# Where the conditioning sums of the last layer run in a four-layer decoder trunk

## The chip, the cores and the metric

The kernel runs on one core of one Trainium2 chip. The metric is the device time of one execution in microseconds (us), as a median of several runs. "PE" is the engine that multiplies matrices, "PEld" its weight loads, "DVE" the vector engine, "ACT" the scalar engine, "POOL" the general engine and "SP" the engine whose queue issues most DMAs. Each engine works through its own instructions in a fixed order; where an instruction waits for another engine, everything behind it on the same engine waits too.

## What is computed

Four layers, each with one token mixer, work on x of 1024 positions by 1024 features, all in 32-bit floats. Ahead of each mixer the input is normalised, scaled and shifted, and behind it the result is multiplied by a gate; scale, shift and gate of a layer come from one conditioning vector c:

```python
for i in range(DEPTH):                                  # DEPTH = 4
    mod = (c @ ada_w[i] + ada_b[i])[:, None, :]         # 1024 -> 3 * 1024
    shift, scale, gate = jnp.split(mod, 3, axis=-1)
    h = rmsnorm(x, norm_g[i]) * (1.0 + scale) + shift
    kind = i % N_MIXERS                                 # 0, 1, 2, 0
    if kind == 0:   y = hgrn2_mixer(h, ...)             # layers 0 and 3
    elif kind == 1: y = swa_mixer(h, ...)               # layer 1
    else:           y = gdn_mixer(h, ...)               # layer 2
    x = x + gate * y
```

The product `c @ ada_w[i]` is what this case calls the conditioning sums of layer i. Layer 0 is HGRN2 (a gated recurrence), layer 1 attention within a window of 128 positions, layer 2 gated DeltaNet, layer 3 HGRN2 again.

## The kernel before

Each layer projects h with large matrix products, mixes, and projects back. A product of two 32-bit floats is made of three passes (L222, L223, L224: high by high, low by high, high by low parts), so each weight tile is loaded from memory by SP (`w_raw`, L191), rounded to its high part on ACT (`w_hi`, L193) and subtracted on DVE to get its low part (`w_lo`, L194). The tiles `w_raw` lie in a pool of three buffers, tagged `raw`.

The conditioning sums are made by `ada(i, parts)`. The 3072 outputs of a layer are cut into 6 parts of 512. For each part eight tiles of 128 by 512 weights are loaded (`ada_w`, 256 KB each, L462, into the same three `raw` buffers), multiplied by the fitting column of c and added up on DVE (`ada_acc`: one TENSOR_SCALAR, L446, then seven SCALAR_TENSOR_TENSOR, L448). DVE then transposes the sum in blocks (L466, into a `raw` buffer again) and reduces it (L467, `ada_red`). When the parts of a call are done, one small product on PE (L470) puts the sums in place in a bank of PSUM, `ada_ps`, and DVE adds the bias from there into `mod` (L474, four instructions, and L492 for the scales). That bank has the tag `tr`, of which there is one; the transposes of the mixers (`kh_ps`, `qt_ps`, `ktr_ps` and others) use the same one bank. The generator `ada` yields after each of the eight loads and after each part, so a part has 9 steps and a half layer (3 parts) 27.

The order of the work around these steps comes from `weave`, which interleaves several generators by estimated shares of the time, and after that from a scheduler that places each engine's instructions by the order written, by what is ready by its estimate, and by which buffers are free. The conditioning sums of the next layer are the stream `side` of the present layer, woven with its mixing and its projections. The table `NS` says how many steps a weave takes:

```python
# hgrn2, for each head h but the last; the first takes 18
weave(self.tc, (mix(h, ds[h]), 16000, 0, 1, PRH), (g, tot, 0, 1, 0), (take(side, ns), ns, 0, 1, 0))
# swa, for each group g of four heads but the last (three times), then what is left
weave(self.tc, (mix(g, ds[g]), 28000, 0, 1, PRS), (chain(proj_q(g + 1, ds[g + 1]), proj_z(g + 1, ds[g + 1])), 42000, 0, 1, 0), (take(side, NS[1]), NS[1], 0, 1, 0))
drain(side)
# gdn, for each pair of heads u (eight times)
weave(self.tc, *st_, (chain(*cs), tot, 0, 1, 0), (take(side, NS[2]), NS[2], 0, 1, 0))
```

In the attention layer `mix(g)` goes through eight blocks of positions. Of each block it transposes the queries into `qt_ps` (L1467, tag `tr`), copies them out on ACT (L1470, L1471, `sw_qhi`) and DVE (L1472, `sw_qlo`), makes the scores (L1483, L1484, `s_ps`), the softmax, and the product with the values (L1511). In the same weave `proj_q` and `proj_z` of the next group run: `proj_q` ends with DVE writing the rotated queries `sw_q` (L1391, two buffers of half the positions each), `proj_z` with ACT and DVE moving its bank of PSUM into `sw_zs` (L1448, L1451). Three banks serve the projections in turn. L1448 needs one of four buffers `sw_tmp`, which L1391 also holds until it is done.

In gated DeltaNet each pair of heads needs projections with a short convolution (L698), an inverse (L845 to L899, with the products `z_ps`) and a scan over eight chunks (`ks_ps`, `w_ps`, `S_ps`).

Of the kernel before, what the change touches and what calls it, by code (L numbers as in the profile page):

```python
# [39 lines left out]

BURST = 4000

NS = 11, 16, 10

ZL = ((2, 1), (3, 0)), ((3, 1),), ((4, 0),), ((4, 1), (5, 0)), ((5, 1),), ((6, 0),), ((6, 1), (7, 0, 1)), ()

# [1 line left out]
def drain(g):  # L48
    for _ in g:
        pass  # L50


def chain(*gs):
    for g in gs:
        yield from g


def take(g, n):
    for _ in range(n):
        c = next(g, None)  # L60
        if c is None:
            return
        yield c


def weave(tc, *streams):

    live = [[g, tot, b, e - b, b, pr] for g, tot, b, e, pr in streams]
    while live:
        s = min(live, key=lambda x: x[4])  # L70
        if s[5]:
            with tc.high_priority(offset=s[5]):
                c = next(s[0], None)
        else:
            c = next(s[0], None)
        if c is None:
            live.remove(s)
        else:
            s[4] += c * s[3] / s[1]


class Trunk:
# [501 lines left out]
    def gdn(self, i, side):  # L584
# [406 lines left out]
        for u in range(U):  # L991
# [11 lines left out]
            else:  # L1003
                self.fill_x(0)
                cs += [self.out_load(od, 0, KT, 0, gp, "tmp", 2, (self.zd, "tb", bufs["tb"])), self.out_mm(i, w_out, 0, KT, 0, on), self.out_load(od, 0, KT, 1, gp, "tmp", 2, (self.zd, "tb", bufs["tb"]))]
                tot += 41600
            weave(self.tc, *st_, (chain(*cs), tot, 0, 1, 0), (take(side, NS[2]), NS[2], 0, 1, 0))
        drain(side)
# [12 lines left out]
    def hgrn2(self, i, side):  # L1021
# [238 lines left out]
        for h in range(H - 1):  # L1260
            ns = 18 if h == 0 else NS[0]
            gs = {0: [(0, "z")], 1: [], H - 2: [(h, "z"), (h + 1, "qfz")]}.get(h, [(h, "z")])
# [84 lines left out]
    def swa(self, i, side):  # L1347
# [82 lines left out]
        def proj_q(g, d, tps=range(4)):  # L1430
            def ev_q(tp, ps):
                hf = tp // 2
                if tp % 2 == 0:
                    d["q"][hf] = tl("q", n=4 * 256)
                    d["ms"] = sp.tile([P, 16], F32, name="q_ms", tag="q_ms", bufs=2)
                sumsq(ps, d["ms"][:, (tp % 2) * 8:(tp % 2) * 8 + 8])
                rotate(tp, ps, cgq, sgq, d["q"][hf][:, (tp % 2) * HT:(tp % 2 + 1) * HT])
                if tp % 2 == 1:
                    nc.vector.tensor_scalar(d["ms"], d["ms"], 1.0 / 64, EPS, ALU.mult, ALU.add)
                    d["rq"][hf] = self.rsqrt(d["ms"], 16, "q", sp)  # L1440

            yield from self.proj_tm(self.load_tm(w_in, g * 256), ev_q, tps)

        def proj_z(g, d):
            for m in range(2):
                def ev_z(hf, ps):
                    th = tl("tmp")
                    nc.scalar.activation(th, ps, AF.Tanh, scale=0.5)  # L1448
                    if m == 0:
                        d["zs"][hf] = tl("zs", n=2 * HT).rearrange("p (m t) -> p m t", m=2)  # L1450
                    nc.vector.scalar_tensor_tensor(d["zs"][hf][:, m, :], th, 1.0, ps, ALU.add, ALU.mult)  # L1451

                c0 = 1536 + g * 256 + m * P
                yield from self.proj_fm(w_in, c0, ev_z)
# [86 lines left out]
        for g in range(G - 1):  # L1541
            weave(self.tc, (mix(g, ds[g]), 28000, 0, 1, PRS), (chain(proj_q(g + 1, ds[g + 1]), proj_z(g + 1, ds[g + 1])), 42000, 0, 1, 0), (take(side, NS[1]), NS[1], 0, 1, 0))
        drain(side)
# [12 lines left out]
@with_exitstack  # L1556
def trunk(ctx: ExitStack, tc: tile.TileContext, x, c, positions, hgrn_lb, ada_w, ada_b, norm_g,
          hg_in_w, hg_out_w, hg_onorm, sw_in_w, sw_out_w, sw_qnorm, sw_knorm, sw_sinks,
          gd_in_w, gd_out_w, gd_conv_w, gd_a_log, gd_dt_bias, gd_onorm, out, layers=(0, 1, 2, 3)):
    ins = dict(x=x, c=c, positions=positions, hgrn_lb=hgrn_lb, ada_w=ada_w, ada_b=ada_b, norm_g=norm_g,  # L1560
               hg_in_w=hg_in_w, hg_out_w=hg_out_w, hg_onorm=hg_onorm, sw_in_w=sw_in_w, sw_out_w=sw_out_w,
               sw_qnorm=sw_qnorm, sw_knorm=sw_knorm, sw_sinks=sw_sinks, gd_in_w=gd_in_w, gd_out_w=gd_out_w,
               gd_conv_w=gd_conv_w, gd_a_log=gd_a_log, gd_dt_bias=gd_dt_bias, gd_onorm=gd_onorm)
    k = Trunk(ctx, tc, ins)
    k.open_norm()
    with tc.tile_pool(name="start", bufs=1, reuse_waits="tile") as sp:
        k.setup(sp)

        x1 = [sp.tile([P, D], F32, name="x_in", tag="x_in1", bufs=NC) for _ in range(NC)]
        sq = sp.tile([P, D], F32, name="x_sq")  # L1570
        x0 = [sp.tile([P, D], F32, name="x_in", tag="x_in0", bufs=NC) for _ in range(NC)]
        k.fetch_x(0, x0)
        ada = []
        for part, bank, col in ((2, ("lev", "ada_row", 2), 0), (0, None, D), (3, ("s", "ada_row", 1), None), (1, None, None)):
            acc = sp.tile([P, HT], F32, name="ada_acc", tag="acc", bufs=3)
            ada.append((layers[0], part, acc, k.ada_load(layers[0], part), bank))
            if layers[0] == 0 and col is not None:
                k.preload(hg_in_w[0], (col,))
        rb = k.norm_stats(0, k.load_x(sp, 0, x0, sq))
        a = k.norm_apply(layers[0], 0, rb)  # L1580
        for n in range(2):
            gs = [k.ada_first(*x) for x in ada[2 * n:2 * n + 2]]
            for g in gs:
                next(g)
            k.step = k.step if n else None
            for g in gs:
                drain(g)
            drain(take(a, KT // 2))
        drain(a)
        k.start = [tc.cur_priority]  # L1590
        k.fetch_x(1, x1)
        ssq = k.load_x(sp, 1, x1, sq)
        k.spill_x(0)
        rb = k.norm_stats(1, ssq)
        k.start.append(tc.cur_priority)
        drain(k.norm_apply(layers[0], 1, rb))
        k.conv_taps(sp)
    k.level_masks()
    k.nst.close()
    for n, i in enumerate(layers):  # L1600
        nxt = layers[n + 1] if n + 1 < len(layers) else None
        k.more = nxt is not None
        side = iter(())
        if n == 0:
            side = k.ada(i, (4, 5))
        if nxt is not None:
            side = chain(side, k.ada(nxt, (0, 1, 2)), k.ada(nxt, (3, 4, 5)))
        body = (k.hgrn2, k.swa, k.gdn)[i % 3](i, side)
        for hf, t in enumerate(body):
            drain(t)  # L1610
            if nxt is None:
                k.store_x(out, hf)
            else:
                if hf == 0:
                    k.open_norm()
                a = k.norm_apply(nxt, hf, k.norm_stats(hf, keep=hf == 0))
                if hf == 0:
                    k.late = a
                else:
                    drain(k.late)  # L1620
                    k.last = a
                    k.nst.close()
# [29 lines left out]
```

## Time and profile before

| what | value |
|---|---|
| runs shown | 2645.78, 2649.27, 2649.19 us; median 2649.19 |
| the profiled execution | 2648.82 us, of which the span from the first to the last instruction is 2647.1 us |
| busy | PE 97%, PEld 77%, DVE 76%, ACT 50%, POOL 6% |
| granted PE clock | 0.992 |
| moved | 244.70 MB read, 60.88 MB written, 115 GB/s over the span |
| conditioning sums beside layer 0 | 64 loads, 120.7 to 466.1 us |
| beside layer 1 | 48 loads, 725.1 to 941.5 us |
| beside layer 2 | 48 loads, 1205.4 to 1719.2 us |

Layer 0 fills the span to about 590 us, attention to about 1056 us, gated DeltaNet to about 2046 us and the second HGRN2 layer the rest. Times in the profile are microseconds from the start of the span unless marked ns. "Busy" of PE counts overlapped products, so a busy PE can still be slower than its best.

### The profile page before, as it was taken

What the parts mean: (1) busy time and instruction counts of PE and PEld (TensorE: products, weight loads), DVE (VectorE), ACT (ScalarE), POOL (GpSimd) and SP (SyncE); (2) the same over time, 40 slices, a digit from 0 to 9 for tenths busy, and PEclk for the clock granted to TensorE, in tenths of its full rate; (3) what the DMA queues carried; (4) which work ended last, traced back from release to release, by engine and by line L of the source; (5) the groups of instructions that cost most, each with busy time, mean ns of one, the idle gap of its engine ahead of it and who ended that gap; (6) DMA issues with size and microseconds to landing.
All of it is one profiled execution on the core that took longest, in us unless ns stands there. A gap on an engine that the chain in (4) does not pass through costs nothing.

```text
span 2647.1 us, 50764 instructions
## 1 busy us (share of the span) xinstructions
PE 2560.9 (97%) x18271; PEld 2041.4 (77%) x18271; DVE 2016.7 (76%) x5651; ACT 1322.4 (50%) x3466; POOL 161.4 (6%) x382
## 2 busy tenths in 40 slices
PE   7999999999999999999999999999899999999998
PEld 4777777688878867777777777778678877787777
DVE  5485788777787878768899989988776837368675
ACT  3343444443464655545666666666544434245452
POOL 0001000011000000101000100110221000000010
PEclk8999999999999999999999999999999999999999
DMA  7333343544233252534444344333585312122343
GB/s 260 95 114 97 108 142 115 166 138 132 67 101 101 73 165 90 149 94 117 105 110 108 102 119 112 93 88 101 175 247 171 116 49 80 40 82 65 123 140 116
DMA packets 387281, 308.91 MB, mean 117 GB/s; under 512 B 74787, under 2 KB 313814, under 8 KB 387030
## 3 DMA queue, kind: packets, MB, share of 16 engines
q1 hardware_dynamic: 374486, 264.77, 34.4%
q0 software_dynamic: 12544, 40.90, 4.9%
q8 instruction: 144, 2.36, 0.4%
q14 instruction: 107, 0.88, 0.1%
HBM read 244.70 MB, written 60.88 MB: 115 GB/s over the span
## 4 chain that ended last, share of the span: by engine, by line
PE 74%; DVE 12%; DMA 5%; ACT 4%; issue 3%; SPq 0%; POOL 0%; DVEq 0%; POOLq 0%; ACTq 0%
PE proj_ps L222 10%; PE proj_ps L224 10%; PE proj_ps L223 10%; PE outp_ps L222 5%; PE outp_ps L223 5%; PE outp_ps L224 4%; PE projw_ps L223 2%; PE projw_ps L222 2%; PE projw_ps L224 2%; DVE gd_tb L698 1%; PE projt_ps L223 1%; PE projt_ps L224 1%; PE projt_ps L222 1%; DVE w_lo L194 1%; PE w_ps L953 1%
## 5 line engine op out<-in xcount | busy, mean ns | idle before, releaser
L222 PE MATMUL proj_ps<-hhi,w_hi 128*128 128x512 f32 x1664 | 676.7, 407 | 3.6 <-ACT gd_tb L696 3.3
L223 PE MATMUL proj_ps<-hlo,w_hi 128*128 128x512 f32 x1664 | 672.7, 404 | 0.0
L224 PE MATMUL proj_ps<-hhi,w_lo 128*128 128x512 f32 x1664 | 672.1, 404 | 0.0
L222 PEld LDWEIGHTS proj_ps<-hhi,w_hi 128*128 128x128 f32 x1664 | 315.0, 189 | 64.6 <-ACT gd_tb L696 5.9
L224 PEld LDWEIGHTS proj_ps<-hhi,w_lo 128*128 128x128 f32 x1664 | 314.7, 189 | 58.1 <-issue 0.4
L223 PEld LDWEIGHTS proj_ps<-hlo,w_hi 128*128 128x128 f32 x1664 | 315.2, 189 | 55.2 <-issue 0.9
L194 DVE TENSOR_TENSOR w_lo<-w_raw,w_hi 128x512 fp32r<-128x512 f32 x344 | 231.4, 677 | 142.3 <-ACT w_hi L193 139.6
L193 ACT CAST w_hi<-w_raw 128x512 fp32r<-128x512 f32 x344 | 209.5, 612 | 260.6 <-PE proj_ps L223 151.3
L222 PE MATMUL outp_ps<-o_hi,w_hi 128*128 128x512 f32 x576 | 230.2, 402 | 9.2 <-ACT o_hi L1323 7.4
L223 PE MATMUL outp_ps<-o_lo,w_hi 128*128 128x512 f32 x576 | 230.3, 400 | 2.4 <-DVE o_lo L1324 2.3
L224 PE MATMUL outp_ps<-o_hi,w_lo 128*128 128x512 f32 x576 | 228.8, 398 | 0.5 <-DVE w_lo L194 0.5
L196 ACT ACTIVATE w_hi<-w_raw,par 128x512 fp32r<-128x512 f32 (+1 forms) x136 | 94.8, 697 | 131.2 <-PE outp_ps L223 93.1
L698 DVE SCALAR_TENSOR_TENSOR gd_tb<-gd_xs,taps,gd_tb 128x512 f32<-128x512 f32 x192 | 146.2, 762 | 15.9 <-ACT gd_tb L696 12.0
L222 PEld LDWEIGHTS outp_ps<-o_hi,w_hi 128*128 128x128 f32 x576 | 109.5, 190 | 33.4 <-ACT o_hi L1323 9.1
L448 DVE SCALAR_TENSOR_TENSOR ada_acc<-ada_w,par,ada_acc 128x512 f32<-128x512 f32 x154 | 115.1, 748 | 21.1 <-DMA ada_w<-in_ada_w_dram 19.9
L223 PEld LDWEIGHTS outp_ps<-o_lo,w_hi 128*128 128x128 f32 x576 | 109.7, 190 | 26.3 <-DVE o_lo L1324 4.4
L197 DVE SCALAR_TENSOR_TENSOR w_lo<-w_raw,par,w_hi 128x512 fp32r<-128x512 f32 (+1 forms) x136 | 97.0, 716 | 41.4 <-ACT w_hi L196 40.7
L224 PEld LDWEIGHTS outp_ps<-o_hi,w_lo 128*128 128x128 f32 x576 | 109.5, 190 | 22.9 <-DVE w_lo L194 1.0
L1315 POOL DMA_DIRECT2D o_in<-od x72 | 38.8, 539 | 1214.9 <-DMA w_raw<-in_hg_out_w_dram 429.2
L222 PE MATMUL projw_ps<-w_hi,hhi 128*128 128x512 f32 x256 | 102.4, 405 | 2.3 <-DVE hg_q L1041 2.3
L223 PE MATMUL projw_ps<-w_lo,hhi 128*128 128x512 f32 x256 | 103.6, 406 | 0.2 <-DVE w_lo L194 0.2
L224 PE MATMUL projw_ps<-w_hi,hlo 128*128 128x512 f32 x256 | 102.2, 400 | 0.0
(429 smaller groups left out, 5365.7 us busy)
## 6 DMA issues: line engine op xcount, KB each, us to landing
ada_w<-in_ada_w_dram SPq DMA_DIRECT2D x160, 256.0 KB, 2.8
w_raw<-in_hg_in_w_dram SPq DMA_DIRECT2D x136, 256.0 KB, 2.8
w_raw<-in_gd_in_w_dram SPq DMA_DIRECT2D x128, 256.0 KB, 3.0
o_in<-od POOLq DMA_DIRECT2D x72, 256.0 KB, 3.5
x<-xd SPq DMA_DIRECT2D x64, 256.0 KB, 4.5
w_raw<-in_gd_out_w_dram SPq DMA_DIRECT2D x64, 256.0 KB, 3.2
xd<-x POOLq DMA_DIRECT2D x48, 256.0 KB, 2.7
w_raw<-in_sw_in_w_dram SPq DMA_DIRECT2D x44, 256.0 KB, 3.0
```

Of the source, the lines that this page charges most:

```text
L193: nc.scalar.copy(hi, raw)
L194: nc.vector.tensor_tensor(lo, raw, hi.bitcast(F32), ALU.subtract)
L196: nc.scalar.activation(hi, raw, AF.Copy, scale=scale)
L197: nc.vector.scalar_tensor_tensor(lo, raw, scale, hi.bitcast(F32), ALU.mult, ALU.subtract)
L222: mm(out, a[0], b[0], start=start, stop=False)
L223: mm(out, a[0], b[1], start=False, stop=False)
L224: mm(out, a[1], b[0], start=False, stop=stop)
L448: self.step = self.nc.vector.scalar_tensor_tensor(acc, w, c, acc, ALU.mult, ALU.add)
L698: last = nc.vector.scalar_tensor_tensor(y, xs[:, j:j + HT], w(j), y, ALU.mult, ALU.add)
L953: nc.tensor.matmul(po[:, hd[a]], dd["u"][a, hf][:, cs], rhs, start=True, stop=True)
L1315: nc.gpsimd.dma_start(t, od[(k0 + k) * P:(k0 + k + 1) * P, sl])
```

## The change

Before, each layer makes the sums of the layer behind it: layer 0 those of layer 1 (with what is left of its own), layer 1 those of layer 2, layer 2 those of layer 3. Now layer 2 makes none. Layer 0 makes also the first half of layer 3's (parts 0 to 2), and layer 1 the second half (parts 3 to 5). The steps per weave are raised to hold the longer streams: 16 for a head of HGRN2, 27 for a group of attention, none in gated DeltaNet.

```diff
-NS = 11, 16, 10
+NS = 16, 27, 0
...
         if n == 0:
             side = k.ada(i, (4, 5))
-        if nxt is not None:
+        if n < 2 and nxt is not None:
             side = chain(side, k.ada(nxt, (0, 1, 2)), k.ada(nxt, (3, 4, 5)))
+            if len(layers) > 3:
+                side = chain(side, k.ada(layers[3], ((0, 1, 2), (3, 4, 5))[n]))
```

In all, 24 loads and their 24 multiplications move from layer 2 to layer 0, and as many to layer 1, with three transposes, three reductions, one L470 and four L474 each. In attention 16 steps a group made 48 of 54, and six were left for `drain`; now three times 27 make all 81, and since 27 steps are just one call of `ada`, each group ends with the small product L470 and its four additions.

The scheduler places most of the program anew. Three places show it.

On DVE, in gated DeltaNet, ahead of the first copy `gd_uq` (L886) that the inverse's products wait for. `gd_tmp` with `gd_cmask` (L817) is work of the next inverse, `gd_q` (L705) of a convolution. Before:

```order
L194 TENSOR_TENSOR w_lo<-w_raw,w_hi 128x512
L817 TENSOR_TENSOR gd_tmp<-gd_tmp,gd_cmask 128x512
L448 SCALAR_TENSOR_TENSOR ada_acc<-ada_w,par,ada_acc 128x512
L886 COPY gd_uq<-z_ps 32x16x32
L887 COPY gd_uq<-z_ps 32x16x32
```

Now:

```order
L817 TENSOR_TENSOR gd_tmp<-gd_tmp,gd_cmask 128x512
L194 TENSOR_TENSOR w_lo<-w_raw,w_hi 128x512
L705 SCALAR_TENSOR_TENSOR gd_q<-gd_tb 128x512
L886 COPY gd_uq<-z_ps 32x16x32
L887 COPY gd_uq<-z_ps 32x16x32
```

The conditioning step is gone from the row ahead of the copy, and another instruction of gated DeltaNet stands there.

On PE, in attention, where the last block of group 0 has its queries transposed (the `qt_ps` rows). `projt_ps` and `proj_ps` are projections of the next group, `pt_ps` and `pv_ps` belong to the block before. Before:

```order
L1505 MATMUL pt_ps<-ident,sw_sm 128x128 x4
L1467 MATMUL qt_ps<-ident,sw_q 64x128 x4
L224 MATMUL projt_ps<-w_hi,hlo 128x256
L222 MATMUL projt_ps<-w_hi,hhi 128x256
L223 MATMUL projt_ps<-w_lo,hhi 128x256
L1511 MATMUL pv_ps<-sw_pth,v 64x256 x4
```

Now:

```order
L222 MATMUL proj_ps<-hhi,w_hi 128x512
L223 MATMUL proj_ps<-hlo,w_hi 128x512
L224 MATMUL proj_ps<-hhi,w_lo 128x512
L470 MATMUL ada_ps<-ada_red,eye_483 128x48
L1467 MATMUL qt_ps<-ident,sw_q 64x128 x4
L1483 MATMUL s_ps<-kst,sw_qhi 128x256 x2
L1467 MATMUL qt_ps<-ident,sw_q 64x128 x3
L1484 MATMUL s_ps<-kst,sw_qlo_7047 128x256
```

The last block's transposes have moved behind the projections of the weave and behind L470, with which they share the one `tr` bank; the second `qt_ps` row is already the first block of the next group, and no projection stands between. The same rows stand at the end of groups 1 and 2. Before, L470 stands directly ahead of `qt_ps` only once, at the end of group 2.

On DVE, at the same end of group 0. Before, from the last block's `sw_qlo` on (L1486 and L1517 are steps of the blocks):

```order
L1472 TENSOR_TENSOR sw_qlo_6956<-qt_ps,sw_qhi 64x512
L448 SCALAR_TENSOR_TENSOR ada_acc<-ada_w,par,ada_acc 128x512 x2
L1486 TENSOR_REDUCE sw_st<-s_ps 128x2
L448 SCALAR_TENSOR_TENSOR ada_acc<-ada_w,par,ada_acc 128x512
L1517 TENSOR_TENSOR sw_of<-pv_ps,sw_zs 128x2x128
L448 SCALAR_TENSOR_TENSOR ada_acc<-ada_w,par,ada_acc 128x512
L1486 TENSOR_REDUCE sw_st<-s_ps 128x2
```

Now:

```order
L446 TENSOR_SCALAR ada_acc<-ada_w,par 128x512
L448 SCALAR_TENSOR_TENSOR ada_acc<-ada_w,par,ada_acc 128x512 x2
L194 TENSOR_TENSOR w_lo<-w_raw,w_hi 128x512 x2
L448 SCALAR_TENSOR_TENSOR ada_acc<-ada_w,par,ada_acc 128x512 x5
L466 STREAM_TRANSPOSE ada_t<-ada_acc 128x512
L467 TENSOR_REDUCE ada_red<-ada_t 128x16
L474 TENSOR_TENSOR mod<-ada_ps,adab 32x12 x4
L1391 TENSOR_TENSOR sw_q<-sw_tmp 128x512 x2
L194 TENSOR_TENSOR w_lo<-w_raw,w_hi 128x512
L1472 TENSOR_TENSOR sw_qlo_7047<-qt_ps,sw_qhi 64x512
L1451 SCALAR_TENSOR_TENSOR sw_zs<-sw_tmp,proj_ps 128x512 x2
```

Before, steps of the blocks and of the sums alternate. Now a whole part of the sums stands in one piece, with only two `w_lo` in it, and behind it, in a row, the queries of the next group, the last block's low part and two banks of the projections.

## The prediction, made before the changed kernel ran

> **What bounds the kernel now.** I read the page's busy times and slices first.
>
> ```profile
> span 2647.1 us, 50764 instructions
> PE 2560.9 (97%) x18271; PEld 2041.4 (77%) x18271; DVE 2016.7 (76%) x5651; ACT 1322.4 (50%) x3466; POOL 161.4 (6%) x382
> PE   7999999999999999999999999999899999999998
> DVE  5485788777787878768899989988776837368675
> PE 74%; DVE 12%; DMA 5%; ACT 4%; issue 3%; SPq 0%; POOL 0%; DVEq 0%; POOLq 0%; ACTq 0%
> ```
>
> PE is busy in nearly every slice and carries 74% of the chain of work that ended last. The change takes no large product away, so it can only move the moments at which PE stands still, 86 us in all (2647.1 less 2560.9). DVE is fullest in slices 19 to 26, in gated DeltaNet. Next, busy times by stretch: attention's three weaves; layer 0's HGRN2 between the same two points as the second HGRN2 layer's (from the transposes of the second half of head 0 to those of the second half of head 6); gated DeltaNet with the sums and behind the last of them.
>
> ```profile
> core 0: us, PE busy (x) PEld busy (x) DVE busy (x) ACT busy (x) POOL busy (x), PEclk, DMA share, GB/s
> 144.20:464.40 320.20, 314.48 (x2915) 248.56 (x2913) 250.09 (x822) 135.75 (x366) 7.25 (x8) 1.00 0.40 117
> 2171.50:2489.70 318.20, 314.99 (x2917) 250.24 (x2917) 210.84 (x754) 132.43 (x364) 0.00 (x0) 1.00 0.23 70
> 726.00:930.00 204.00, 200.44 (x1420) 165.90 (x1419) 169.84 (x521) 116.77 (x311) 0.00 (x0) 1.00 0.31 91
> 1254.00:1716.00 462.00, 450.19 (x3251) 360.89 (x3249) 424.02 (x1217) 297.48 (x950) 41.00 (x105) 1.00 0.42 106
> 1716.00:1848.00 132.00, 130.77 (x843) 104.43 (x843) 114.34 (x362) 83.51 (x270) 8.34 (x22) 0.97 0.38 98
> ```
>
> PE idles 5.72 of 320.2 us in layer 0, 3.21 of 318.2 in layer 3, which makes no sums, 3.56 of 204 (1.75%) in attention, 11.81 of 462 (2.56%) in gated DeltaNet, and 1.23 of 132 (0.93%) there without sums. DVE is 92% full in gated DeltaNet, 83% in attention, 78% in layer 0.
>
> **What moves.** One step of the sums costs these (ns, minimum, median, maximum):
>
> ```profile
> L448 DVE SCALAR_TENSOR_TENSOR ada_acc<-ada_w,par,ada_acc x154: 714/750/756, 21.9 to 1725.4; 128x512 f32<-128x512 f32 x154
> L446 DVE TENSOR_SCALAR ada_acc<-ada_w,par x22: 477/482/489, 21.3 to 1636.0; 128x512 f32<-128x512 f32 x22
> L466 DVE STREAM_TRANSPOSE ada_t<-ada_acc x20: 691/708/714, 145.5 to 1727.4; 128x512 f32<-128x512 f32 x20
> L467 DVE TENSOR_REDUCE ada_red<-ada_t x20: 667/680/686, 146.5 to 1729.3; 128x16 f32<-128x512 f32 x20
> ada_w<-in_ada_w_dram SPq DMA_DIRECT2D x160, 256.0 KB, 2.8
> ```
>
> Half a layer is 3 of L446, 21 of L448 and 3 each of L466 and L467: 1.45 + 15.75 + 2.12 + 2.04 = 21.4 us of DVE. Gated DeltaNet loses 42.8; HGRN2 layer 0 and attention gain 21.4 each. SP's queue issues 24 loads of 256 KB more in each, 48 fewer in gated DeltaNet. How long DVE waited for these loads, beside layer 0, attention and gated DeltaNet in that order:
>
> ```profile
>   DMA ada_w<-in_ada_w_dram: 17.3, 14
>   DMA ada_w<-in_ada_w_dram: 6.5, 10
>   DMA ada_w<-in_ada_w_dram: 1.0, 2
> ```
>
> These are 0.27 us a load in layer 0 (64 loads) and 0.14 in attention (48), so DVE there gains 6.5 and 3.3 us of waiting. Attention's weaves have 34.2 us of DVE to spare and keep 9.5; layer 0 has 70. Two L470 and eight L474 move too; they are priced with the place where they land. POOL's queue is passed by nothing that moves.
>
> *Gated DeltaNet, freed.* Two bounds. With sums PE idles 2.56%, without them 0.93%; over the 520 us that hold the sums the difference is 8.5 us, if all of it is theirs. The other bound is layer 0 against layer 3: 2.51 us more idle, with DVE work of sums as large as this:
>
> ```profile
> 144.20:464.40 320.20, 0.00 (x0) 0.00 (x0) 44.03 (x62) 0.00 (x0) 1.00 0.40 117
> ```
>
> That is 0.057 us of idle PE for each us of sums, so 42.8 us are worth 2.4. Nothing excludes zero, since the rest is reordered. What PE waits for in this layer decides between the bounds:
>
> ```profile
> PE z_ps L891 <- DVE gd_uq L886: 5.6, 5, 1.6
> PE vtr_ps L711 <- DVE gd_tb L705: 1.8, 4, 1.0
> 1241.06 0.74 DVE L448 SCALAR_TENSOR_TENSOR ada_acc<-ada_w,par,ada_acc 128x512 f32<-128x512 f32 x1
> 1241.83 0.69 DVE L886 COPY gd_uq<-z_ps 32x512 f32<-32x512 f32 x1
> 1242.66 0.94 PE L891 MATMUL z_ps<-gd_Z,gd_uq 64*64 64x64 f32 x25 [1.60 <-DVE gd_uq L886]
> ```
>
> The largest wait is for L886, five times, and in one of them a step of the sums ran ahead of the copy, 0.74 of its 1.60 us. In the order of before the other copies have no such step directly ahead, and in the new order another instruction has taken that place. So I stay nearer to the lower bound: a gain of 4 us, between 0 and 8.5. What is late next are the same copies, behind `gd_cmask` and the convolutions.
>
> The Trainium skill (Perfetto Trace Analysis, "Identifying the Most-Contended Engine") holds that busy time of matmuls misleads, since they are pipelined, and that PE's headroom is read from weight loads. By its measure PE is at 78.1% in gated DeltaNet with sums and 79.1% without, against 77.6% and 78.6% in the two HGRN2 stretches, so 1.0 point of 78.1 over 520 us, 6.7 us, would be the gain, 1.0 of 77.6 over 320 us, 4.1 us, the price of 44 us of sums and 2.0 that of 21.4, and the sum below would be -6.7 + 2.0 + 2.0 + 7.8 = 5.1 instead of 6.2.
>
> *HGRN2 layer 0, loaded.* At 0.057 a us, 21.4 us cost 1.2; at least nothing, at most the 2.5 that 44 us cost now. SP's loads and the three `raw` buffers are the cover; DVE's 70 idle us are what keeps it.
>
> *Attention, loaded.* For the fuller DVE alone 1.2 by the same price. If its idle rate went to gated DeltaNet's it would be 1.7 (0.81% of 204).
>
> *Attention, the end of each group.* Here a wait is added. In the new order the sums' last part, L470, the last block's `qt_ps` and then the next group's first block follow each other on PE with no projection between, at three places. L470 is ready only when DVE has done its part; `qt_ps` waits for the `tr` bank until L474 has read it; the scores wait for ACT's and DVE's copies. Behind L474 on DVE wait `sw_q`, `sw_qlo` and `sw_zs`, and with `sw_zs` the banks of the next projections, so PE has nothing else to take. The order of before has this once, at the end of group 2:
>
> ```profile
> 954.55 0.32 PE L470 MATMUL ada_ps<-ada_red,eye 128*128 128x48 f32 x2
> 955.75 0.60 PE L1467 MATMUL qt_ps<-ident,sw_q 128*64 128x128 f32 x4 [0.89 <-DVE mod L474]
> 957.60 0.44 PE L1483 MATMUL s_ps<-kst,sw_qhi 128*128 128x128 f32 x2 [1.26 <-ACT sw_qhi L1471]
> 958.32 0.33 PE L1484 MATMUL s_ps<-kst,sw_qlo 128*128 128x128 f32 x1 [0.28 <-DVE sw_qlo L1472]
> ```
>
> PE idles 0.89 + 1.26 + 0.28 = 2.4 us. `sw_qlo` now has two `sw_q` and a `w_lo` ahead of it, which fit into the time that ACT needs, so I keep 2.4. Ahead of L470 nothing was waited for then, because the part had been done 6 us before. Now it is the last thing on DVE, and this is its pace (first step, a step five before the end, and the reduction):
>
> ```profile
> 935.28 0.49 DVE L446 TENSOR_SCALAR ada_acc<-ada_w,par 128x512 f32<-128x512 f32 x1 [1.06 <-DMA ada_w<-in_ada_w_dram]
> 939.54 0.75 DVE L448 SCALAR_TENSOR_TENSOR ada_acc<-ada_w,par,ada_acc 128x512 f32<-128x512 f32 x1
> 947.74 0.69 DVE L467 TENSOR_REDUCE ada_red<-ada_t 128x16 f32<-128x512 f32 x1
> 949.79 0.39 PE L222 MATMUL proj_ps<-hhi,w_hi 128*128 128x512 f32 x1
> 954.32 0.39 PE L224 MATMUL proj_ps<-hhi,w_lo 128*128 128x512 f32 x1
> ```
>
> In the new order the last five steps, transpose and reduction stand behind the `w_lo` that frees PE's last projection of 24 products. The five took 8.9 us here (939.54 to 948.43), though with other work between; the projection takes 24 times 0.227 (20 spacings from 949.79 to 954.32), 5.4. So PE waits between 0 and 3.5 us ahead of L470; I take 1.0, since without that other work five steps and both others come to 5 times 0.75 + 1.39 = 5.1, about 5.4, and only waits for loads add to it. One end of a group then costs 3.4, three cost 10.2, and the 2.4 that stand there today go: 7.8. The least, if PE takes other work at two of them, is 0; the most, with 3.5 at each, 3 times 5.9 less 2.4, is 15.3.
>
> Sum: -4 + 1.2 + 1.2 + 7.8 = +6.2 us, on 2648.82 of the profiled execution 2655.0. The median of the runs shown is 0.4 higher, so the forecast is 2655.4. With every term at its lower bound it is -8.5, with every term at its upper one 0 + 2.5 + 1.7 + 15.3 = +19.5.
>
> **The rivals.** The bound from which a measurement of this kernel can tell a change is about 0.2%, 5.3 us; on it "slower" begins at 2654.5.
>
> *Faster: gated DeltaNet gives its upper bound and the ends of groups cost nothing.* For it speaks that DVE is fullest there and that PE is 99% busy once the sums are done; against it, that work differs there (no convolution of another pair of heads), and that four of five waits for L886 had no step ahead. It needs PE to be served at the ends of two groups by projections that the new order does not have there: -8.5 + 1.2 + 1.2 = -6.1, 2643.1. It decides once gated DeltaNet gains 5.3 us more than attention loses.
>
> *No change to be told: the ends of groups cost only what the copies cost.* If PE never waits ahead of L470, and each of the two new places costs 2.4, attention's is 4.8, and the sum +3.2: 2652.4. For it speaks that PE's last projection and DVE's last five steps are nearly equally long.
>
> *Much slower: the loads pace the ends of groups.* Eight loads and two weights go through three buffers, each 2.8 us from issue to landing, which is what paced 935.28 to 948.43. With 3.5 us at each of three places the sum is -4 + 2.4 + 15.3 = +13.7: 2662.9.
>
> **How the numbers follow.** The forecast (slower by 5.3 to 10) has 0.38, the loads' pace 0.13, no change to be told 0.33, faster 0.16. Faster is 0.16, within 0.2% 0.33, slower 0.51. The slower case alone reaches from 2654.5 to 2663. Leaving out one in ten at each side: below, what the faster case holds under its own 2643.1, so 2642.5; above, what the loads' pace holds over its 2662.9, so 2664.
>
> **What would show each step.** In the changed profile: `ada_acc` between 120 and 950 us only; PE idle in gated DeltaNet down by 0 to 8.5 us; layer 0 between the same transposes within 3 us of 320.2. At the ends of the three groups, rows of L470, L1467, L1483 with idle times near 0.9 and 1.3 us and `mod` and `sw_qhi` as releasers, and a wait for `ada_red` (L467) ahead of L470. The prediction is wrong if PE has no idle time there, if L470 waits over 3.5 us, or if gated DeltaNet changes by more than 8.5 us; also if reordering elsewhere moves more than these, as it may by about the 2 us by which layers 0 and 3 differ.

## The result, and the profile after

The changed kernel took 2685.26 us (median of 5 runs, 2677.87 to 2690.26) against 2649.19 before (median of 5, 2645.78 to 2651.03): ratio 1.0144, 95% interval 1.013 to 1.0157. That is 36 us slower where 6 were forecast: the direction was right, the size six times too small, and outside the range.

The page of the changed kernel, the lines that answer to those of before:

```profile
span 2679.8 us, 50786 instructions
PE 2574.6 (96%) x18271; PEld 2051.9 (77%) x18271; DVE 2026.8 (76%) x5651; ACT 1320.9 (49%) x3466; POOL 158.1 (6%) x382
PE 70%; DVE 15%; DMA 6%; ACT 4%; issue 3%; SPq 1%; POOL 0%; DVEq 0%; ACTq 0%; POOLq 0%
```

PE's share of the chain fell from 74% to 70%, DVE's rose from 12% to 15%. PE idles 105.2 us (2679.8 less 2574.6) instead of 86.2, which accounts for 19.0 of the 32.7 us of span. The other 13.7 us are a *longer* busy time of PE, for the same 18271 products. That is a kind of loss that the prediction had no term for.

Where it lies is read from busy times by stretch. First attention and gated DeltaNet before (from the first column sum of a layer's norm, L518, to the next):

```profile
core 0: us, PE busy (x) PEld busy (x) DVE busy (x) ACT busy (x) POOL busy (x), PEclk, DMA share, GB/s
623.40:1022.50 399.10, 391.19 (x2607) 324.92 (x2606) 307.75 (x861) 205.28 (x508) 10.81 (x20) 1.00 0.33 102
1088.40:2042.10 953.70, 925.23 (x6079) 740.37 (x6077) 805.33 (x2138) 561.40 (x1649) 104.48 (x244) 1.00 0.46 125
```

and after, with HGRN2 layer 0 between the same transposes as in the prediction (320.20 us there) ahead of them:

```profile
144.70:479.60 334.90, 319.19 (x2921) 251.22 (x2920) 268.71 (x855) 134.78 (x365) 7.26 (x8) 0.99 0.42 128
633.60:1056.80 423.20, 399.09 (x2608) 330.60 (x2607) 326.34 (x896) 205.15 (x508) 11.00 (x20) 0.97 0.36 111
1122.80:2074.00 951.20, 926.12 (x6074) 742.02 (x6072) 775.93 (x2069) 560.43 (x1649) 100.88 (x244) 0.99 0.41 112
```

Layer 0 lost 14.7 us in this stretch, 10.0 of them idle time of PE (5.72 to 15.71) and 4.7 busy time (314.48 to 319.19). Its tail gave some back: the first L518 behind it stands at 584.0 instead of 573.7, 10.3 later. Attention lost 24.1, of which 16.2 is idle time of PE (7.9 to 24.1) and 7.9 busy time, at a mean clock of 0.97. Gated DeltaNet gave 2.5. The remainder moved by under 1 us.

What PE waited for in attention, the first rows (total, times, longest):

```profile
PE ada_ps L470 <- DVE ada_red L467: 6.8, 3, 3.1
PE s_ps L1483 <- ACT sw_qhi L1471: 3.8, 3, 1.3
PE qt_ps L1467 <- DVE sw_qlo L1472: 2.8, 5, 0.7
PE qt_ps L1467 <- DVE mod L474: 2.7, 3, 0.9
```

They are waited for once at each of the three ends of groups; `sw_qlo` twice more, 0.3 us each, in the first block behind an end. The end of group 1 on PE, from the last projection on:

```profile
883.39 0.39 PE L223 MATMUL proj_ps<-hlo,w_hi 128*128 128x512 f32 x1
883.62 0.39 PE L224 MATMUL proj_ps<-hhi,w_lo 128*128 128x512 f32 x1
887.08 0.42 PE L470 MATMUL ada_ps<-ada_red,eye 128*128 128x48 f32 x2 [3.08 <-DVE ada_red L467]
888.39 1.03 PE L1467 MATMUL qt_ps<-ident,sw_q 128*64 128x128 f32 x4 [0.89 <-DVE mod L474]
890.69 0.80 PE L1483 MATMUL s_ps<-kst,sw_qhi 128*128 128x256 f32 x2 [1.26 <-ACT sw_qhi L1471]
892.22 0.82 PE L1467 MATMUL qt_ps<-ident,sw_q 128*64 128x128 f32 x3 [0.74 <-DVE sw_qlo L1472]
...
896.09 0.63 PE L222 MATMUL proj_ps<-hhi,w_hi 128*128 128x512 f32 x1
896.52 0.63 PE L223 MATMUL proj_ps<-hlo,w_hi 128*128 128x512 f32 x1
```

The chain of waits is the one foretold, with 0.89 and 1.26 us to the digit. Two things differ: 3.08 us ahead of L470 (1.0 was taken) and 0.74 for `sw_qlo` (0.28 was kept). And the last two rows show what comes behind: the same product, 0.23 us from start to start before the gap (883.39 to 883.62), follows at 0.43 us (896.09 to 896.52). The stretches around this end have the granted clock:

```profile
883.00:892.50 9.50, 3.53 (x15) 2.11 (x14) 7.26 (x15) 3.62 (x7) 0.00 (x0) 0.73 0.37 108
892.50:897.00 4.50, 4.50 (x18) 3.77 (x17) 3.41 (x8) 1.40 (x3) 0.00 (x0) 0.50 0.19 56
907.00:917.00 10.00, 9.89 (x80) 8.50 (x81) 8.86 (x28) 6.56 (x23) 0.00 (x0) 1.00 0.53 168
```

While PE was busy for 3.53 of 9.5 us the clock fell, and for the next 4.5 us it stood at 0.50; later it is back at 1.00. The Trainium skill (TensorE: Matmul & The Clock Gate, "What's actually happening") says that the array's clock is gated to half after an idle window of about 3.4 us and comes back after a busy one; half is what this trace grants, and the prediction did not weigh that rule.

### The profile page after: what moved, and what is told of

Same layout as the page of the kernel before. It is cut to its first block, busy times and chain, and to the rows that moved or that the text cites. A ratio compares the mean times of both kernels' runs of the same rounds, so it can differ in the third digit from the quotient of the medians.

```text
span 2679.8 us, 50786 instructions
## 1 busy us (share of the span) xinstructions
PE 2574.6 (96%) x18271; PEld 2051.9 (77%) x18271; DVE 2026.8 (76%) x5651; ACT 1320.9 (49%) x3466; POOL 158.1 (6%) x382
## 4 chain that ended last, share of the span: by engine, by line
PE 70%; DVE 15%; DMA 6%; ACT 4%; issue 3%; SPq 1%; POOL 0%; DVEq 0%; ACTq 0%; POOLq 0%
PE proj_ps L224 9%; PE proj_ps L222 9%; PE proj_ps L223 9%; PE outp_ps L222 5%; PE outp_ps L224 5%; PE outp_ps L223 5%; DMA ada_w<-in_ada_w_dram 2%; PE projw_ps L223 2%; PE projw_ps L222 2%; PE projw_ps L224 2%; DVE gd_tb L698 1%; DVE w_lo L194 1%; PE projt_ps L223 1%; PE projt_ps L222 1%; PE projt_ps L224 1%
```

## The experiments

In one table, read from each kernel's profile in the same way: the time at which layer 0 ends (first L518), the lengths of attention and of gated DeltaNet, and the ratio to the kernel before in the same comparison. "Sums" are those of layer 3 unless said otherwise.

| kernel | layer 0 ends | attention | gated DeltaNet | median | ratio (95%) |
|---|---|---|---|---|---|
| before | 573.7 | 399.1 | 953.7 | 2649.19 | |
| after | 584.0 | 423.2 | 951.2 | 2685.26 | 1.0144 (1.013 to 1.0157) |
| hg_only | 586.4 | 402.6 | 951.0 | 2661.97 | 1.0047 (1.0034 to 1.0061) |
| sw_only | 572.7 | 427.9 | 953.1 | 2676.76 | 1.0098 (1.008 to 1.0117) |
| ns25 | 586.2 | 413.8 | 953.5 | 2668.78 | 1.0076 (1.0055 to 1.0097) |
| defer | 593.9 | 408.8 | 951.9 | 2671.80 | 1.0082 (1.0058 to 1.0106) |
| sw_fix | 584.5 | 410.0 | 949.9 | 2663.75 | 1.0061 (1.0044 to 1.0079) |
| b_ns27 | 572.9 | 423.8 | 949.6 | 2669.17 | 1.0081 (1.0064 to 1.0098) |
| sw_light | 583.2 | 409.8 | 944.5 | 2664.48 | 1.0077 (1.0058 to 1.0096) |
| sw_noload | 586.0 | 409.8 | 946.5 | 2667.11 | 1.0075 (1.006 to 1.009) |
| hg_load | 584.0 | 399.3 | 955.6 | 2663.27 | 1.0054 (1.0039 to 1.0069) |
| hg_dve | 583.6 | 401.3 | 948.3 | 2660.47 | 1.0046 (1.0029 to 1.0063) |
| hg_light | 575.4 | 425.3 | 945.2 | 2671.18 | 1.0101 (1.0081 to 1.0122) |
| hg_noload | 572.6 | 426.8 | 944.2 | 2667.71 | 1.0081 (1.0066 to 1.0096) |
| pdq | 587.8 | 426.9 | 952.5 | 2690.70 | 1.0171 (1.0153 to 1.0189) |
| b_pdq | 581.5 | 398.4 | 953.1 | 2657.60 | 1.0042 (1.0027 to 1.0057) |
| sw_load | 573.0 | 426.8 | 949.1 | 2672.91 | 1.0090 (1.0075 to 1.0105) |
| sw_dve | 574.0 | 425.9 | 954.9 | 2676.49 | 1.0103 (1.0088 to 1.0118) |

Gated DeltaNet differs by up to 9 us between executions that issue the same instructions in it, so a kernel's median is no measure of a few us in another layer; the lengths of the layers are.

**Each half alone.** Is the loss the sum of two places?

```diff
-NS = 16, 27, 0
+NS = 16, 16, 5        # hg_only
+            side = chain(side, k.ada(layers[3], ((0, 1, 2), (), (3, 4, 5))[n]))
+NS = 11, 27, 5        # sw_only
+            side = chain(side, k.ada(layers[3], ((), (0, 1, 2), (3, 4, 5))[n]))
```

> Only the first half of layer 3's sums (parts 0 to 2) is moved, beside HGRN2 layer 0 (16 steps per head from head 1 on); the second half stays beside gated DeltaNet (5 steps per chunk pair), attention keeps 16 steps per group. Theory A (each place pays for its own sums: layer 0 lost 10.3 us between the two traces, attention 24, gated DeltaNet gave 2.5): +10 in layer 0, 0 in attention, -1 in gated DeltaNet, so about 2658 us. Theory B (the loss in layer 0 only arises with the other half's transfers or is noise between two profiles; the price on record, 1.2 us): 2649 to 2651 us.

> Only the second half (parts 3 to 5) is moved, beside attention (27 steps per group); the first half stays beside gated DeltaNet (5 steps per chunk pair), HGRN2 layer 0 keeps 11 steps per head. Theory A: layer 0 as before, attention +24, gated DeltaNet -1, so about 2672 us. Theory B (attention's loss follows from a granted clock that HGRN2 layer 0's fuller stretch has already pulled down): attention +14 at most, 2662 us or less.

(In sw_only it is parts 0 to 2 that stand beside attention and 3 to 5 beside gated DeltaNet; the halves are of one size.) In hg_only layer 0 lost 12.7 us and attention 3.5; in sw_only layer 0 lost nothing and attention 28.8. Theory A holds in so far as the two places lose separately, and attention without any help from layer 0. Each of these kernels has both the added sums and the raised number of steps, so they don't tell which of the two costs.

**The ends of attention's groups.** Three edits take the end of a call away from the end of a group: 25 steps in place of 27; L470 issued four steps into the next call, in all layers; the same beside attention only.

```diff
-NS = 16, 27, 0
+NS = 16, 25, 0        # ns25
```

```diff
             for k in range(KT):
...
                 self.ada_step(acc, wt, k)
+                if k == 3:
+                    self.ada_fin()   # L470, L474 of the call before
                 yield 1
...
         drain(side)
+        self.ada_fin()
```

> The changed kernel with 25 in place of 27 steps per group of attention, so that the calls of 27 steps no longer end where the groups end; the last 6 steps run behind the third group. Theory A1 (the ends of calls at the ends of groups are what costs: PE waits for ada_red ahead of L470 and then for the transposes' bank, while no projection of the next group is left to fill in): two of three ends move into the middle of a group, attention's loss falls from 24 to 10 or less, plus 6 steps uncovered behind the last group (6 x 1.5 us = 9 if all are exposed): 2670 to 2680 us, and the idle time of L470 in groups 1 and 2 below 1 us. Theory A2 (it is the mass of sums, DVE being fuller and its loads in the weights' buffers): 2683 us or more, with the same idle time spread over the groups.

> The changed kernel, but the one matmul of L470 and the four additions behind it are issued four steps into the next call of the sums (behind the last call: after the drain), in every layer. Theory A1: the wait for ada_red ahead of L470 (1.8 to 3.2 us at each of three ends) goes, and with it the wait of the next transposes for the bank; 3 x 6 us idle and the slower clock behind them: 2658 to 2666 us. Theory A2: at the group's end it is the queue on DVE that is late (the normalised queries' low parts stand behind the sums), so the same time is waited ahead of the scores instead: 2680 us or more.

> The changed kernel with the one matmul of L470 and the additions behind it issued four steps into the next call of the sums, but only for the three calls that run beside attention; HGRN2 layer 0 is as in the changed kernel. Theory A1 (ends of groups): attention takes 409 us between its two layer ends in place of 423 (as it did in 'defer'), layer 0 keeps its loss of 10: 2668 to 2673 us, and a granted clock of 1.00 behind the ends of groups 0 and 1. Theory A2: no better than 2680 us.

Attention fell from 423.2 to 413.8, 408.8 and 410.0 us. In ns25 14.7 us of the loss remain (10 or less were expected, and up to 9 more for the steps behind the last group): the first two ends have no wait for `ada_red` left, but the six steps behind the last group make PE wait 8.2 us once ahead of L470. In sw_fix no wait ahead of L470 is left. It came out 4 us below its range, since the two medians are 21.5 us apart where the two profiles are 14.4; the profile's attention, 13.2 us shorter, is as expected. Busy times by stretch around the ends of groups 0, 1 and 2 in sw_fix:

```profile
780.00:800.00 20.00, 18.26 (x107) 12.21 (x107) 19.33 (x65) 11.34 (x32) 0.00 (x0) 1.00 0.39 112
800.00:815.00 15.00, 15.00 (x74) 11.34 (x73) 12.36 (x28) 7.25 (x18) 0.00 (x0) 1.00 0.56 167
880.00:900.00 20.00, 19.26 (x112) 14.38 (x108) 15.28 (x39) 10.15 (x28) 0.00 (x0) 1.00 0.56 169
960.00:985.00 25.00, 19.59 (x81) 15.31 (x80) 15.54 (x31) 9.66 (x18) 3.78 (x7) 0.86 0.58 186
```

Behind the first two ends the clock stays at 1.00; the third, where no next call of the sums exists to defer into, still idles 5.41 of 25 us and slows. In defer the deferral in HGRN2 cost layer 0 another 10 us, which puts the kernel over its range (2671.80 where 2658 to 2666 were expected); why L470 costs more in the later place stays open.

Are the added sums needed for this loss? b_ns27 is the kernel before with one number changed; it makes the same 54 steps beside attention, but both calls end with a group.

```diff
-NS = 11, 16, 10
+NS = 11, 27, 10
```

> The kernel before with 27 in place of 16 steps per group of attention: the same 54 steps, none added, but both calls now end where groups 0 and 1 end, and group 2 has none. Theory A1 (the coincidence costs, 7 to 9 us at each end with the slower clock behind it): attention +14 to +18, less what the third group gains without sums (its end in the kernel before, 2.5 us): 2660 to 2665 us. Theory A2 (the loss needs the added sums): 2652 us or less.

Attention took 423.8 us, 24.7 more than before, with no sum added: more than the expected 14 to 18. Its two ends, by stretch (the wait and what follows it, for groups 0 and 1):

```profile
791.00:798.00 7.00, 2.76 (x14) 1.67 (x12) 5.56 (x13) 3.85 (x7) 0.00 (x0) 0.82 0.43 115
798.00:803.00 5.00, 5.00 (x20) 4.16 (x19) 3.44 (x9) 1.16 (x2) 0.00 (x0) 0.57 0.14 49
876.70:885.70 9.00, 2.90 (x12) 1.56 (x12) 6.67 (x14) 3.56 (x7) 0.00 (x0) 0.73 0.32 104
885.70:891.00 5.30, 5.30 (x19) 4.44 (x18) 3.77 (x10) 1.45 (x3) 0.00 (x0) 0.50 0.18 52
```

10.3 us of idle time (4.24 and 6.10) and a clock of 0.57 and 0.50 behind it, from two ends. Not all of the 24.7 us are theirs: the clock stands at 0.50 also in the layer's first 4.8 us, in 3.4 us from 771.6 and in 6.8 us from 996.8, where PE is busy for 4.80, 3.08 and 6.52 us, and half of that, about 7 us, is an estimate of what it costs. So it is partly chance that this total equals the changed kernel's. What the run shows is that ends of calls at ends of groups cost this with no sum added: most of attention's loss is set by the step count, 27, which is also the length of a call, and not by the 27 steps that were added to 54.

What is late at the end: VectorE's copies, or the loads? sw_light keeps the loads of all three calls beside attention and cuts seven of eight copies to 16 elements; sw_noload keeps the copies and loads nothing.

```diff
-                self.ada_step(acc, wt, k)
+                n = 16 if k and (i == 2 or (i, p0) == (3, 3)) else HT
+                self.ada_step(acc[:, :n], wt[:, :n], k)
```

> The changed kernel, but in all three calls of the sums beside attention VectorE does the first of eight steps of a part in full and the other seven on 16 of 512 elements (these sums left out); loads, transposes, reductions and L470 stay where they are. If VectorE's copies pace the ends of groups: PE's waits ahead of L470 fall from 6.8 us to 2 or less, attention from 423 to 412 us or less. If the loads pace them: L470's waits stay at 5 us or more and attention at 420 or more. Either way the waits behind L470 (for mod, sw_qhi, sw_qlo) stay.

> The changed kernel, but all three calls of the sums beside attention multiply a resident tile instead of loading 72 tiles (not the right sums); the copies stay. If the loads pace the ends: L470's waits 2 us or less, attention 412 us or less. If the copies pace them: 5 us or more, and 420 us or more.

Attention is 409.8 us in both (in sw_noload one of the nine parts is done ahead of the layer), and ahead of L470 PE's weight load waits for `ada_red` 0.5 us once in sw_light and never in sw_noload. So taking away either is enough, and neither alone paces the end: the last part is late because VectorE takes the copies in order and stands behind their loads, as at the end of group 1 of the changed kernel:

```profile
882.77 1.54 DVE L448 SCALAR_TENSOR_TENSOR ada_acc<-ada_w,par,ada_acc 128x512 f32<-128x512 f32 x2 [1.28 <-DMA ada_w<-in_ada_w_dram]
884.81 0.75 DVE L448 SCALAR_TENSOR_TENSOR ada_acc<-ada_w,par,ada_acc 128x512 f32<-128x512 f32 x1 [0.50 <-DMA ada_w<-in_ada_w_dram]
885.60 0.71 DVE L466 STREAM_TRANSPOSE ada_t<-ada_acc 128x512 f32<-128x512 f32 x1
```

The waits behind L470 did stay, as expected: 2.7 us for `mod`, 3.9 for `sw_qhi`, 1.7 for `sw_qlo` in sw_light. With the 2.4 of before taken off they are 5.9 us, and PE's busy time is 4.5 us longer (395.68 against 391.19): 10.4 of the 10.7 us by which 409.8 stands over 399.1.

sw_load and sw_dve had been meant for this question. Their edits took effect on the half that stayed beside gated DeltaNet, so they say nothing of attention; it kept its 426 to 427 us.

> As sw_only, but of layer 3's second half VectorE does only the first of eight steps of a part in full, the other seven on 16 of 512 elements (these sums left out); loads, ada_t, ada_red and L470 stay. Theory V (at the ends of groups VectorE's queue is late: copies of the sums of 0.75 us stand ahead of ada_red, sw_qlo and the rest): the ends shrink only at the one call that is layer 3's (the third); attention's loss of 28 us falls by the third end's 7 us and the fuller stretches of its group, to 18 to 22: 2666 to 2670 us. Theory R (the loads pace it): 2674 us or more.

> As sw_only, but layer 3's second half multiplies a resident tile instead of loading its 24 tiles (not the right sums). Theory R: the last group's end is no longer paced by loads, 2670 us or less. Theory V: L470 in the third end is still reached by PE before ada_red, 2674 us or more.

**HGRN2 layer 0.** The largest gap of PE there, at 382 us, with the SyncE queue at that time (PE row, then the queue's):

```profile
385.70 0.79 PE L222 MATMUL proj_ps<-hhi,w_hi 128*128 128x512 f32 x1 [3.81 <-ACT w_hi L193]
...
380.22 1.78 SPq L1227 DMA_DIRECT2D pd<-hg_tmp  x4
382.09 0.95 SPq L191 DMA_DIRECT2D w_raw<-in_hg_in_w_dram  x2
```

The weights' loads were issued behind the stores of a head's outputs (L1227), and of the queue's waits between 355 and 396 us the longest is theirs:

```profile
SPq L1227 <- DVE hg_S L1212: 13.0, 1, 13.0
```

(The 4.1 us of the expectations are all of this product's waits for `w_hi` on the page; this one is 3.81.) That suggested a cause, theory Q, and with it an edit: those stores on GpSimd's queue.

```diff
-                        nc.sync.dma_start(dst[a], ob[a * 32:(a + 1) * 32]...
+                        nc.gpsimd.dma_start(dst[a], ob[a * 32:(a + 1) * 32]...
```

> The changed kernel with the stores of the normalised outputs (L1227) issued on GpSimd's queue instead of SyncE's. Theory Q (in HGRN2 layer 0 the loss is the weights' loads standing behind a store that waits up to 13 us at the head of SyncE's queue, with the halved clock behind that gap): the gap of 4.1 us at 382 us goes, layer 0 ends 5 to 8 us earlier, 2677 to 2680 us. Theory V (the loss is VectorE's, its own work standing behind the sums' copies): layer 0 as in the changed kernel, 2683 us or more. Against both: stores on the other queue cost more per issue, and layer 3 (which has the same stores and no sums) would show it.

> The kernel before with the stores of L1227 on GpSimd's queue. If these stores hold back loads in the kernel before as well (33 us of waits of SyncE's queue at L1227 in both HGRN2 layers), 2643 to 2647 us; if the loads are early enough there, 2649 us, no change.

Q's numbers did not come true. In pdq the gap at 382 us is gone, yet the stretch between the transposes is as long as in the changed kernel (334.9 us) and the layer ends 3.8 us later. In the kernel before the same edit cost 7.8 us in layer 0, which neither number for b_pdq had allowed for. So the edit has a price of its own, and pdq can't refute Q: with the stores on GpSimd's queue the change makes layer 0 end 6.3 us later (581.5 to 587.8) instead of 10.3. Up to 4 us may be Q's, if that price is the same in both kernels; the rest of the loss is there without the gap.

The other two suspects are VectorE's copies and the loads of the sums. hg_load and hg_dve took each away from layer 3's half alone, which runs last in the layer:

> As hg_only, but of layer 3's first half VectorE does only the first of eight steps of a part in full and the other seven on 16 of 512 elements (so these sums are left out); all 24 loads into the weights' three buffers stay, as do ada_t, ada_red and L470. Theory R (the ring of three raw buffers: the weights' loads queue behind the sums' loads and behind ada_t, as at 382 to 386 us, where PE waits 4.1 us for w_hi): most of hg_only's loss in layer 0 (12.7 us) stays, 2658 us or more. Theory V (VectorE fuller by 21 steps of 0.75 us = 16 us, its own work late): 2652 us or less.

> As hg_only, but layer 3's first half multiplies a tile that is resident instead of loading its 24 tiles (so these sums are not the right ones): VectorE's work is all there, the 24 loads and their places in the ring are gone (ada_t keeps its 3). Theory R: 2652 us or less. Theory V: 2658 us or more.

Layer 0 ended at 584.0 and 583.6, 2.4 and 2.8 us earlier than in hg_only. Most of the loss stays in both, so each run speaks against the theory that the other supports. The sums stand in one chain, layer 1's first, and 16 steps a head make *those* denser: in the changed kernel 13.7 of PE's 15.7 us of idle time lie ahead of 404.0 us, where the first of layer 3's sums is multiplied. (The direct test of that rate, the kernel before with 16 steps a head and no sum added, was not run.) To reach those sums, hg_light and hg_noload, on the changed kernel, act on every call that starts from the second head on:

> The changed kernel, but of the calls that start from the second head of HGRN2 layer 0 on (layer 1's, and layer 3's first half) VectorE does the first of eight steps of a part in full and the other seven on 16 of 512 elements (these sums left out); loads, ring and queue are unchanged. Theory V: VectorE loses 63 copies of about 0.65 us, layer 0 is back at its old length or below, 10 us or more earlier: 2675 us or less. Theory Q: the loads pace it, layer 0 ends within 3 us of the changed kernel: 2682 us or more.

> The changed kernel, but the calls that start from the second head of HGRN2 layer 0 on (layer 1's, and layer 3's first half) multiply a resident tile instead of loading 72 tiles (not the right sums); VectorE's copies are all there. Theory V (VectorE's own time): layer 0 ends within 3 us of the changed kernel's 584 us; 2680 us or more. Theory R (the loads' places in SyncE's queue and in the ring of three buffers, which light copies had freed earlier): layer 0 ends 6 us earlier or more, near 575; 2677 us or less.

```diff
-                wt = self.wp.tile([P, HT], F32, name="ada_w", tag="raw", bufs=RAW)
-                nc.sync.dma_start(wt, w[:, k, part * HT:(part + 1) * HT])
+                if i == 1 or (i, p0) == (3, 0):      # hg_noload
+                    wt = self.hhi[0][:, 0, :].bitcast(F32)
+                else:
+                    ...                               # tile and load as before
                 self.ada_step(acc, wt, k)
```

Light copies brought the layer's end to 575.4, no loads to 572.6, where the kernel before has 573.7. Theory V (VectorE's own time) falls with the second: all the copies are there. Theory R's number came true, and the first run doesn't contradict it, since R supposes that light copies free the three buffers earlier. What both runs show together is that the loss needs the loads and the full copies at once. Between the transposes, hg_light:

```profile
145.00:469.40 324.40, 315.70 (x2918) 248.53 (x2916) 239.77 (x849) 134.95 (x365) 7.25 (x8) 1.00 0.44 130
```

and hg_noload:

```profile
142.80:465.10 322.30, 314.82 (x2918) 248.83 (x2917) 272.58 (x863) 135.04 (x366) 7.25 (x8) 1.00 0.27 80
```

VectorE's waits at the sums' copies between the same points, in the kernel before:

```profile
DVE ada_acc L448 <- DMA ada_w<-in_ada_w_dram: 13.0, 11, 2.8
```

after:

```profile
DVE ada_acc L448 <- DMA ada_w<-in_ada_w_dram: 16.9, 16, 2.8
DVE ada_acc L446 <- DMA ada_w<-in_ada_w_dram: 5.6, 5, 2.6
```

and in hg_light:

```profile
DVE ada_acc L448 <- DMA ada_w<-in_ada_w_dram: 17.8, 14, 3.8
DVE ada_acc L446 <- DMA ada_w<-in_ada_w_dram: 6.6, 3, 3.8
```

One measure sets the changed kernel apart: VectorE's busy time plus the time for which it is blocked by a copy of the sums whose tile has not landed. It is 250.1 + 13.0 = 263 us before, 268.7 + 22.5 = 291 after, 239.8 + 24.4 = 264 in hg_light and 272.6 + 2.1 = 275 in hg_noload; PE idles 5.7, 15.7, 8.7 and 7.5 us. Only the kernel in which both add up loses much; the last two are not in order. In b_pdq no copy is added, but the blocked time grows to 27.2 us, and the sum to 281:

```profile
144.80:473.00 328.20, 316.19 (x2918) 249.73 (x2917) 253.58 (x825) 138.22 (x369) 33.45 (x56) 0.99 0.39 116
PE lev_ps L1125 <- DVE hg_X L1148: 10.6, 8, 2.8
```

PE idles 12.0 us there, most of it for VectorE's own work (`hg_X`). Between the same transposes of all 18 kernels, seven have a sum of 262 to 275 us, and PE idles 5.6 to 8.7; eleven have 281 to 295 us, and PE idles 12.0 to 18.2. So the measure tells the two groups apart, but it remains a reading. ACT, which rounds the weights, waits longer for their loads as well, before and after:

```profile
ACT w_hi L193 <- DMA w_raw<-in_hg_in_w_dram: 13.2, 11, 3.2
ACT w_hi L193 <- DMA w_raw<-in_hg_in_w_dram: 38.0, 16, 8.2
```

It is 17.2 us in hg_light and 8.0 in hg_noload, where the loss is nearly gone, but also only 15.2 in b_pdq, where PE idles 12.0. Of the waits of PE in the changed kernel 7.7 us are for VectorE (4.3 before), 3.8 for `w_hi` (none before) and 3.5 for other work of ACT (0.3 before). What the loss owes to VectorE's blocked queue, and what to weights that come late, stays open, and so does the share of the queue's order in the gap at 382 us.

No kernel here beats the one before; of those that do all the work the nearest are b_pdq (1.0042) and hg_only (1.0047).

## Why the prediction was right or wrong

By the two profiles the kernel became 32.7 us longer where +6.2 was forecast. Of the 26.5 us between, attention has 15.1, layer 0 9.1, gated DeltaNet 1.5 and the rest 0.8. Two steps failed: the price of the sums in layer 0, and the price of an end of a group, which was too low in idle time and had nothing for the clock.

- **Gated DeltaNet, -4 us (0 to -8.5).** Inside its bounds: 2.5 in the two profiles, with 3.4 us less idle time of PE. The runs can't tell it from nothing: nine kernels without sums there average 948.8 us and three with all of them 952.1, 3.3 apart, inside a spread of 9.
- **The end of each group, 3.4 us at three places, +7.8.** The mechanism was right in place, order and releasers, and the term was mis-sized. Ahead of L470 6.8 us are waited in all, 2.3 an end where 1.0 was taken; the choice rested on five copies, transpose and reduction running without a wait for a load, and the rows at 882.77 and 884.81 show such waits (1.28 and 0.50). The copies cost 9.3 (3.8 + 2.8 + 2.7, with the 0.6 a block behind the ends) and not 7.2, since `sw_qlo` did not fit into ACT's time at 0.74 a place. That makes 13.7 us of idle time with the 2.4 of before taken off, where 7.8 was taken, inside the bounds (0 to 15.3).
- **The missing term: the clock behind an end.** PE's busy time in attention grew by 7.9 us for the same products. The sum had priced idle time only. 13.7 + 7.9 = 21.6 of attention's 24.1. Layer 0 has the same in small: 4.7 of its 14.7 us between the transposes are busy time.
- **Attention's fuller DVE, +1.2.** At most the 2.5 us that the last two points leave, so not contradicted. b_ns27 has none of the added sums and lost as much, if in part elsewhere.
- **HGRN2 layer 0, +1.2 (0 to 2.5), "within 3 us of 320.2".** Wrong: 334.9 between the transposes, 10.3 at the layer's end. The failed step is the price of 0.057 us of idle PE for each us of sums, an average over the sums that the layer had, used for the next 21.4 us: PE idled 10.0 us more, 0.47 a us. VectorE still idles 66.2 of the 334.9 us, so its idle time was not the cover for which the prediction took it. The profile held the warning: 17.3 us of waits for `ada_w` in layer 0, and the prediction even worked out 6.5 more; it then called the loads a cover and priced them at nothing. VectorE's blocked time rose by 9.5, its busy time by 18.6, and without either of them the loss is gone; by which way the delay reaches PE stays open.
- **Rivals.** "Much slower: the loads pace the ends of groups" was the nearest, with 3.5 us at each end (measured 1.66 to 3.1) and no term for the clock or for layer 0. Faster and no change are excluded by the interval.
- **What was named as showing it wrong** did: layer 0 outside its 3 us. L470 stayed below 3.5.

## What to carry to other kernels

An average price from a profile (idle PE per us of added work) need not be the price of the next piece where an engine takes its work in order and may be blocked at the head of its queue: add its busy and its blocked time before you count on what is left. When a side stream is dealt out in equal portions, see that a portion's length is not that of its closing dependence; one number, 16 to 27, made attention 24.7 us longer without an added sum, and in the changed kernel issuing the closing product four steps later gave 13 back. And where PE loses several us within ten, count the products behind the gap at half speed, too.

## What the hardware showed that was not expected

The clock halved without one long gap. At the end of group 0 of the changed kernel no idle stretch of PE is longer than 1.66 us, but four come within 7 us (1.66, 0.89, 1.26 and 0.74). The first of them, and then the clock by stretch:

```profile
799.93 0.42 PE L470 MATMUL ada_ps<-ada_red,eye 128*128 128x48 f32 x2 [1.66 <-DVE ada_red L467]
```

```profile
797.50:800.00 2.50, 0.84 (x5) 0.38 (x3) 2.15 (x3) 0.21 (x1) 0.00 (x0) 1.00 0.52 133
800.00:803.00 3.00, 0.95 (x6) 0.59 (x6) 1.79 (x6) 1.52 (x3) 0.00 (x0) 0.84 0.53 152
803.00:806.00 3.00, 2.16 (x9) 1.73 (x10) 2.65 (x5) 2.12 (x5) 0.00 (x0) 0.50 0.30 90
810.00:812.00 2.00, 2.00 (x13) 1.66 (x11) 0.00 (x0) 1.29 (x5) 0.00 (x0) 1.00 0.42 131
394.00:398.00 4.00, 2.29 (x14) 1.67 (x13) 2.88 (x6) 2.25 (x7) 0.00 (x0) 1.00 0.63 179
```

The clock is at 0.50 from 803 us on and back at 1.00 by 810; it went down within the second row, where PE is busy for 0.95 of 3 us. The last row, from layer 0, has 1.71 us of idle time in 4 us, in one gap, and keeps 1.00. So in these two places the sparse stretch counted, not its longest gap. The Trainium skill (TensorE: Matmul & The Clock Gate, "Why this matters for your kernels") advises to have no gap over about 3 us between bursts; at this end shorter ones, close together, did the same.
